# Second attention branch begun ahead of its gate's projections, a pair every eight weight tiles, and five tiles between block transpose and split

## The chip, the cores and the metric

The kernel runs on one core of a Trainium2 chip. The metric is the device time of one execution in microseconds. Three runs of the kernel before took 1014.35, 1013.31 and 1014.84 us (median 1014.35).

## The reference

One decoder layer over 256 tokens of width 2048, in fp32. A normalized input is multiplied by one wide matrix, whose columns feed three gated branches and three merge gates.

```
h = rmsnorm(x, norm_g)
proj = h @ w_in                      # qa ka va ga | qb kb vb gb | xc gc | mg
ya = moba_attention(qa, ka, va)      # branch A: 8 heads of 128, causal over 256
yb = swa_attention(qb, kb, vb)       # branch B: 16 query heads of 64, 4 key heads, window 128, sinks
yc = rglru_branch(xc)                # branch C: convolution, gated linear recurrence
y = [ya * silu(ga), yb * silu(gb), yc * silu(gc)]
merged = sum(sigmoid(mg) * (y[b] @ w_br[b]))
x = x + merged @ w_out
x = x + sigmoid(rmsnorm(x) @ w_pg) * (p @ w_pp)
return rmsnorm(x, final_norm_g)
```

Both attentions add a relative-position bias to their logits. For 256 tokens branch A has one block and so is plain causal attention.

## The kernel before

All weights stream from memory in tiles of 128 x 1024 fp32 (512 KB): 232 of `w_in`, 48 of `w_br`, 32 of `w_out`, 32 of `w_pg`, 4 of `w_pp`. Each product keeps its precision by splitting both operands into a high and a low part: ScalarE casts a tile to the high part (`wh`, L118), VectorE subtracts to get the low part (`wl`, L119), and TensorE multiplies high by high, high by low and low by high (`mm3`, L150 to L152, or L212 and L214 where the output is wanted feature-major). There are four raw tiles and four split tiles, so the cast of a tile waits until TensorE has done with the tile four places earlier, and TensorE runs at most some tiles behind the splits. SyncE issues the weight loads, in order.

The order of the big stages is: branch C's projections, branch A's projections with branch C's recurrence between, the merge of C, branch B's projections, the merge of A, the merge of B, the output projection, the last gate. The small work of the two attentions is not in a stage of its own. It is cut into steps (generators) that `hand_out` (L131) puts on a list, and `tick` (L122) takes one entry from the list after every weight tile that is split. `period` is the number of ticks from one pair of heads to the next, `STEPS` the number of ticks that a pair's generator needs, and `drain` (L127) runs what is left. A scheduler then lays the instructions of each engine in an order; weight splits have a priority ahead of the steps.

A pair of branch B (`pair`, L661) does this, a line for each step:

- step 0: for an even pair, load the bias of four heads (ScalarE's queue) and split keys and values (`head_group`, L647)
- step 1: split the queries (`q_b`, L669 and L670), scores on TensorE (`s_b`, L523)
- step 2: add the bias and take the maximum (L539, L541)
- step 3: exponential on ScalarE (L553), then `AHEAD` = 4 ticks of nothing
- step 7: normalize (L562), transpose in blocks of 32 on VectorE (`flip_b`, L569), send to DRAM (`d_b`, L571) and fetch back as four blocks (`turn_b`, L574) on SyncE, then `LATE` ticks of nothing
- then: split the probabilities (`w_b`, high part on ScalarE L598, low part on VectorE L599) and multiply with the values on TensorE (`py_b`, L523)
- last step: put the heads together (L689, L691), multiply with the gate (L693), split the result (L226, L227)

Branch A's pairs (`pair`, L610) have the same form with a period of 11 ticks over the merge of C (48 tiles), and use the same `LATE` and `STEPS`. Before, branch B's pairs are handed out after its gate's projections (`silu`, L731) with a period of 6, over the 48 tiles of the merge of A, and run into the first tiles of the merge of B. In the merge of A each of four column blocks ends with a product on VectorE (`sg_a`, L792) and an add on GpSimd (`merged`, L793); the next block begins with 8 tiles of `w_in`, then 4 of `w_br`.

Of the kernel before, what the change touches and what calls it, by code (L numbers as in the profile page):

```python
# [28 lines left out]
NB, DB = 16, 64  # L29
# [10 lines left out]
WPAD = 64  # L40
QD = 32
AHEAD = 4
STEPS = 13
LATE = 3
TURN_LATE = 5
WOFF = 32
RV = 384
# [3 lines left out]
def trunk(ctx: ExitStack, tc: tile.TileContext, x, xt, p, table, onehot, maskv, w_in, sinks, conv, w_ri, vec, fin, w_br,  # L51
# [14 lines left out]
    def ktiles(t):  # L66
        return t[:, : KB * SEQ].rearrange("p (k t) -> p k t", k=KB)

    def cols(k, n=1):
        return slice(k * SEQ, (k + n) * SEQ)  # L70

    def aux(name):
        return ps_x.tile([P, CW], F32, tag="aux", name=name)

    def temp(name):
        return small.tile([P, 4, SEQ], F32, tag="tmp", name=name, bufs=4)
# [54 lines left out]
    def hand_out(works, period):  # L131

        end = object()
        live = []

        def step():
            live[:] = [g for g in live if next(g, end) is not end]

        def begin(g):
            live.append(g)  # L140
            step()

        for g in works:
            todo.append(lambda g=g: begin(g))
            todo.extend([step] * (period - 1))
        todo.extend([step] * (STEPS - period))

# [69 lines left out]
    def unit(name):  # L217
        return block(f"{name}_hi", F32R), block(f"{name}_lo", F32R)
# [212 lines left out]
    def bias_tile(h0, n, name):  # L431
        t = small.tile([P, 4, 2 * P], F32, tag="bias", name=name)
        nc.scalar.dma_start(t[:, :n], bass.AP(tensor=rv_d.tensor, offset=rv_d.offset + h0 * RV, ap=[[1, P], [RV, n], [1, 2 * P]]))
        return t
# [9 lines left out]
    def turned(dst, n, factor=None):  # L444
        for c in range(n):
            scaled(dst[:, 2 * c : 2 * c + 2, :], in_turned(), factor)

    def silu(dst, n, name):
        for c in range(0, n, 2):
            d = dst[:, 2 * c : 2 * c + 4, :]  # L450
            turned(d, 2)
            s = temp(f"sig_{name}{c}")
            nc.scalar.activation(s, d, AF.Sigmoid)
            nc.vector.tensor_tensor(d, d, s, op=ALU.mult)
# [61 lines left out]
    def chained(calls):  # L516
        ins = None
        for call in calls:
            with tc.issue_after(ins) if ins is not None else nullcontext():
                ins = call().ins  # L520

    def mm(out, a, b, start, stop):
        return lambda: nc.tensor.matmul(out, a, b, start=start, stop=stop)  # L523

    def probs(name):
        return small.tile([P, 3, 2, P], F32, tag="e", name=name, bufs=2)
# [37 lines left out]
    def flip(dst, srcs, n, name):  # L564

        t = temp(f"flip_{name}").rearrange("p k t -> p (k t)")[:, : n * P]
        view = t.rearrange("p (b m q) -> p m b q", b=4, m=n)
        for at, src in srcs:
            nc.vector.transpose(view[:, at], src.rearrange("p (m b q) -> p m b q", b=4, q=QD))  # L569
        d = dram.tile([P, n * P], F32, tag=f"flip{n}", name=f"d_{name}", bufs=4)  # L570
        nc.sync.dma_start(d, t)  # L571
        back = d.rearrange("(a i) (b c) -> b i a c", a=4, b=4)
        for b in range(4):
            nc.sync.dma_start(dst[quad[b]].rearrange("i (a c) -> i a c", a=4), back[b])  # L574
# [4 lines left out]
    def turned_probs(es, name, out):  # L579
        t = temp(f"turn_{name}").rearrange("p k t -> p (k t)")[:, : 6 * P]  # L580
        flip(t, [(slice(0, 6), es.rearrange("p k j t -> p (k j t)"))], 6, name)
        for _ in range(LATE):
            yield
        out.append(flipped(t, 6))

    def softmax_steps(es, scs, bias, mx, den, name, out, sk=None, sink=None):
        softmax_max(es, scs, bias, mx, sk, sink)
        yield
        softmax_exp(es, mx, den, sk)
        for _ in range(AHEAD):  # L590
            yield
        softmax_norm(es, den, sk)
        yield from turned_probs(es, name, out)

    def split_probs(t, n, name):
        w = small.tile([P, 2, 6 * P], F32R, tag="w", name=name)[:, :, : n * P]
        hi, lo = (w[:, i].rearrange("p (m a q) -> p m a q", m=n, a=4) for i in range(2))
        nc.scalar.copy(hi, t[:, :n])  # L598
        nc.vector.tensor_tensor(lo, t[:, :n], hi.bitcast(F32), op=ALU.subtract)  # L599
        return [w[:, i] for i in range(2)]  # L600

    def by_head(w, n=2):
        return w[:, : n * SEQ].rearrange("p (k j t) -> p j k t", k=n, j=2)
# [37 lines left out]
    def attention_pairs(qb, kb, vt, gate):  # L641
        z = unit("zb")
        mx, den, sk = (small.tile([P, NB, NH], F32, tag=f"st{i}b", name=f"st{i}b", bufs=1) for i in range(3))
        half = [slice(j * DB, (j + 1) * DB) for j in range(2)]
        shared = {}

        def head_group(g):  # L647
            bias = bias_tile(NA + 4 * g, 4, f"bias_b{g}")
            src, own = kb[g // 2][half[g % 2]], g % 2
            ks = small.tile([P, 2, SEQ], F32R, tag="s", name=f"k_b{g}")  # L650
            nc.scalar.copy(ks[half[0], 1, :], src)
            nc.scalar.copy(ks[half[1], 0, :], src)
            for j in range(2):
                nc.vector.tensor_tensor(ks[half[j], j, :], src, ks[half[own], 1 - own, :].bitcast(F32), op=ALU.subtract)
            vs = small.tile([P, NH, 2, DB], F32R, tag="v", name=f"v_b{g}")
            vsrc = vt[:, :, g * DB : (g + 1) * DB]
            nc.scalar.copy(vs[:, :, 0, :], vsrc)
            nc.vector.tensor_tensor(vs[:, :, 1, :], vsrc, vs[:, :, 0, :].bitcast(F32), op=ALU.subtract)
            shared[g] = bias, ks, vs.rearrange("p c s d -> p c (s d)")

        def pair(i):  # L661
            pr = slice(2 * i, 2 * i + 2)
            if i % 2 == 0:
                head_group(i // 2)
            yield
            bias, ks, vc = shared[i // 2]
            qs = small.tile([P, 2, SEQ], F32R, tag="q", name=f"q_b{i}")
            for j in range(2):
                nc.scalar.copy(qs[half[j], j, :], qb[i][half[j]])  # L669
                nc.vector.tensor_tensor(qs[half[1 - j], j, :], qb[i][half[j]], qs[half[j], j, :].bitcast(F32), op=ALU.subtract)  # L670
            scs = [aux(f"s_b{i}{j}") for j in range(2)]
            early = [sc[:, SEQ:].rearrange("p (s t) -> p s t", s=2) for sc in scs]
            chained([mm(scs[j][:, :SEQ], qs[:, j, P:], ks[:, j ^ n, :], n == 0, n == 1) for j in range(2) for n in range(2)]
                    + [mm(early[j], qs[:, j, :P], ks[:, :, :P], True, True) for j in range(2)])
            es = probs(f"e_b{i}")
            yield
            out = []
            yield from softmax_steps(es, scs, bias[:, i % 2 * 2 : i % 2 * 2 + 2], mx[:, pr], den[:, pr], f"b{i}", out,
                                     sk[:, pr], sinkb[:, pr])
            w = split_probs(out[0], 6, f"w_b{i}")  # L680
            py = aux(f"py_b{i}")
            pj = py.rearrange("p (j k t) -> p j k t", j=2, k=2)
            last = [t[:, 4 * P :].rearrange("p (j t) -> p j t", j=2) for t in w]
            chained([mm(pj, vc[:, 0], by_head(w[1 - n]), n == 0, False) for n in range(2)]
                    + [mm(pj[:, :, 1], vc[:, 1], last[1 - n], False, n == 1) for n in range(2)])
            yield
            y = qb[i]
            for j in range(2):
                nc.scalar.copy(y[half[j]], py[half[1 - j], j * SEQ : (j + 1) * SEQ])  # L689
            for j in range(2):  # L690
                nc.vector.tensor_tensor(y[half[j]], py[half[j], j * SEQ : (j + 1) * SEQ], y[half[j]], op=ALU.add)  # L691
            gi = gate[:, cols(i)]
            nc.vector.tensor_tensor(gi, y, gi, op=ALU.mult)  # L693
            split_act(z, i, 1, gi)

        hand_out([pair(i) for i in range(NB // 2)], 6)
        return z

    def token_values(dst, ps, c0):
# [24 lines left out]
    def branch_b():  # L724
        qT, kv, g = block("qb"), block("kvb"), block("gb")
        turned(ktiles(qT), 4, DB ** -0.5)
        kT = ktiles(kv)[:, :2, :]
        vt = ktiles(kv)[:, 2:4, :]
        turned(kT, 1)
        token_values(vt, in_chunk(NKV * DB), 0)  # L730
        silu(ktiles(g), 4, "gb")  # L731

        qb = [ktiles(qT)[:, i, :] for i in range(NB // 2)]
        kb = [kT[:, i, :] for i in range(2)]
        return attention_pairs(qb, kb, vt, g)

    merged = []
    mT = []
# [223 lines left out]
```

## Time and profile before

| | |
|---|---|
| median of three runs | 1014.35 us |
| profiled execution | 1014.71 us, span 1012.9 us |
| mean granted TensorE clock | 0.996 |
| TensorE busy | 995.3 us (98%) |
| VectorE busy | 673.1 us (66%) |
| ScalarE busy | 549.1 us (54%) |
| HBM traffic | 216.4 MB, 214 GB/s over the span |

How to read it: TensorE's matmuls overlap, so the time of one is told by the distance from its start to the next start (about 0.23 us for 512 columns), not by its duration. A number in brackets behind a row is how long the engine stood idle before it and what ended that. A wait on an engine that is not the bottleneck costs nothing unless TensorE later waits for that engine. The stages in this profile: branch A's pairs run from 286 to 431 us, branch B's projections from 431 to 543 us with the gate's 16 tiles from 498.8, the merge of A from 543.4 to 697, the merge of B up to 828 us.

### The profile page before, as it was taken

To read this page: it belongs to the slowest core of one execution; us is meant where nothing else is said; L and a number is where in the kernel's file an instruction comes from. 1 tells how busy PE (TensorE), PEld (TensorE's weight loads), DVE (VectorE), ACT (ScalarE), POOL (GpSimd) and SP (SyncE) were. 2 spreads that over 40 slices of the span, in tenths; PEclk is the share of its full clock that TensorE was granted. 3 is DMA by queue.
4 is the path that set the end of the run, shared out by engine and by line. 5 is a ranking of instruction groups with operands and counts; after the bars stand their busy time and mean duration, and the time that the engine had idled before them with its cause. 6 is when DMAs were issued, how large, how long until landed. Compare 5 with 4: busy or idle time off the path is not lost.

```text
span 1012.9 us, 13571 instructions
## 1 busy us (share of the span) xinstructions
PE 995.3 (98%) x5024; PEld 845.1 (83%) x5024; DVE 673.1 (66%) x993; ACT 549.1 (54%) x767; POOL 15.1 (1%) x14
## 2 busy tenths in 40 slices
PE   9999999999999999999999998999999999999996
PEld 7888888888888888888988877788788888888886
DVE  6766956667867576555456787697656555565764
ACT  8644455557555556544446756766544444454552
POOL 0000000000000000000000001010000000000000
PEclk9999999999999999999999999999999999999999
DMA  9856656554666766666656657867677786779662
GB/s 338 305 190 220 197 187 180 174 177 157 209 208 205 224 209 195 210 198 191 186 190 199 207 188 207 249 190 240 212 238 231 233 283 207 248 259 326 206 192 83
DMA packets 71977, 216.43 MB, mean 214 GB/s; under 512 B 8120, under 2 KB 21352, under 8 KB 71400
## 3 DMA queue, kind: packets, MB, share of 16 engines
q1 hardware_dynamic: 65376, 202.93, 62.3%
q10 hardware_dynamic: 6536, 12.65, 3.6%
q8 instruction: 39, 0.64, 0.3%
q14 instruction: 26, 0.21, 0.1%
HBM read 202.93 MB, written 12.62 MB: 213 GB/s over the span
## 4 chain that ended last, share of the span: by engine, by line
PE 83%; DMA 5%; DVE 5%; issue 2%; ACT 2%; SPq 1%; POOLq 0%; POOL 0%; ACTq 0%; DVEq 0%
PE ps_in L212 21%; PE ps_in L214 11%; PE ps_in L150 8%; PE ps_in L152 8%; PE ps_in L151 8%; DMA turn_b<-d_b 3%; PE ps_out L150 3%; PE ps_out L151 3%; PE ps_out L152 3%; PE ps_pg L151 3%; PE ps_pg L150 3%; PE ps_pg L152 3%; DMA d_b<-flip_b 2%; PE ps_brc L152 1%; PE ps_brc L150 1%
## 5 line engine op out<-in xcount | busy, mean ns | idle before, releaser
L119 DVE TENSOR_TENSOR wl_in<-r_in,wh_in 128x1024 fp32r<-128x1024 f32 x232 | 284.5, 1228 | 177.3 <-ACT wh_in L118 176.8
L118 ACT CAST wh_in<-r_in 128x1024 fp32r<-128x1024 f32 x232 | 242.7, 1049 | 245.8 <-PE ps_in L212 140.6
L212 PE MATMUL ps_in<-h,wh_in 128*128 128x512 f32 x928 | 290.2, 393 | 0.0
L214 PEld LDWEIGHTS ps_in<-h,wl_in 128*128 128x128 f32 x928 | 173.6, 188 | 39.5
L151 PE MATMUL ps_in<-wl_in,h 128*128 128x512 f32 (+1 forms) x480 | 184.1, 383 | 0.6 <-DVE wl_in L119 0.6
L152 PE MATMUL ps_in<-wh_in,h 128*128 128x512 f32 (+1 forms) x480 | 184.4, 384 | 0.0
L214 PE MATMUL ps_in<-h,wl_in 128*128 128x256 f32 x928 | 184.4, 280 | 0.0
L150 PE MATMUL ps_in<-wh_in,h 128*128 128x512 f32 (+1 forms) x480 | 184.3, 384 | 0.0
L212 PEld LDWEIGHTS ps_in<-h,wh_in 128*128 128x128 f32 x928 | 142.5, 188 | 0.4
L151 PEld LDWEIGHTS ps_in<-wl_in,h 128*128 128x128 f32 x480 | 90.5, 189 | 18.4 <-DVE wl_in L119 1.5
L152 PEld LDWEIGHTS ps_in<-wh_in,h 128*128 128x128 f32 x480 | 90.4, 188 | 17.6
L150 PEld LDWEIGHTS ps_in<-wh_in,h 128*128 128x128 f32 x480 | 90.6, 189 | 17.0
L119 DVE TENSOR_TENSOR wl_out<-r_out,wh_out 128x1024 fp32r<-128x1024 f32 x32 | 38.8, 1223 | 25.7 <-ACT wh_out L118 25.7
L119 DVE TENSOR_TENSOR wl_pg<-r_pg,wh_pg 128x1024 fp32r<-128x1024 f32 x32 | 38.9, 1222 | 25.2 <-ACT wh_pg L118 25.0
L151 PE MATMUL ps_pg<-wl_pg,x_hi 128*128 128x512 f32 (+1 forms) x160 | 55.3, 347 | 0.0
L152 PE MATMUL ps_pg<-wh_pg,x_lo 128*128 128x512 f32 (+1 forms) x160 | 55.3, 347 | 0.0
L150 PE MATMUL ps_pg<-wh_pg,x_hi 128*128 128x512 f32 (+1 forms) x160 | 55.3, 347 | 0.0
L118 ACT CAST wh_out<-r_out 128x1024 fp32r<-128x1024 f32 x32 | 33.4, 1051 | 35.9 <-PE ps_out L152 29.9
L118 ACT CAST wh_pg<-r_pg 128x1024 fp32r<-128x1024 f32 x32 | 33.4, 1052 | 32.1 <-PE ps_pg L152 24.7
L150 PE MATMUL ps_out<-wh_out,m_hi 128*128 128x512 f32 x128 | 49.9, 390 | 0.0
L152 PE MATMUL ps_out<-wh_out,m_lo 128*128 128x512 f32 x128 | 49.8, 389 | 0.0
L151 PE MATMUL ps_out<-wl_out,m_hi 128*128 128x512 f32 x128 | 49.8, 389 | 0.0
(250 smaller groups left out, 1237.6 us busy)
## 6 DMA issues: line engine op xcount, KB each, us to landing
r_in<-w_in_dram SPq DMA_DIRECT2D x232, 512.0 KB, 4.2
r_out<-w_out_dram SPq DMA_DIRECT2D x32, 512.0 KB, 4.3
r_pg<-w_pg_dram SPq DMA_DIRECT2D x24, 512.0 KB, 5.1
r_brc<-w_br_dram SPq DMA_DIRECT2D x16, 512.0 KB, 3.6
r_bra<-w_br_dram SPq DMA_DIRECT2D x16, 512.0 KB, 4.1
r_brb<-w_br_dram SPq DMA_DIRECT2D x16, 512.0 KB, 4.7
r_pg<-w_pgt_dram SPq DMA_DIRECT2D x8, 512.0 KB, 3.3
d_b<-flip_b SPq DMA_DIRECT2D x8, 384.0 KB, 3.5
```

Of the source, the lines that this page charges most:

```text
L118: casts.append(nc.scalar.copy(hi[:, c], r[:, c]).ins)
L119: los.append(nc.vector.tensor_tensor(lo[:, c], r[:, c], hi[:, c].bitcast(F32), op=ALU.subtract).ins)
L150: nc.tensor.matmul(ps, ah, bh, start=first, stop=False)
L151: nc.tensor.matmul(ps, ah, bl, start=False, stop=False)
L152: nc.tensor.matmul(ps, al, bh, start=False, stop=last)
L212: nc.tensor.matmul(ps[:, j, :], wh[:, cs[j]], h_both[k], start=k == 0, stop=False)
L214: nc.tensor.matmul(ps[:, j, SEQ:], wl[:, cs[j]], h_act[k][0], start=False, stop=k == KD - 1)
```

## The change

Two numbers change: `STEPS` from 13 to 14 and `LATE` from 3 to 5, so that a pair waits five ticks, not three, from its block transpose to its split; this holds for both attentions. The call of `attention_pairs` stands before the gate's projections `silu(ktiles(g), 4, "gb")`, so the first ticks of branch B's pairs fall in those 16 tiles, and the period of its pairs is 8 ticks, not 6. A pair's last step, which needs the gate, comes 13 ticks after its first, when the gate's first half has been projected.

```diff
-STEPS = 13
-LATE = 3
+STEPS = 14
+LATE = 5
@@ attention_pairs
-        hand_out([pair(i) for i in range(NB // 2)], 6)
+        hand_out([pair(i) for i in range(NB // 2)], 8)
         return z
@@ branch_b
         token_values(vt, in_chunk(NKV * DB), 0)
-        silu(ktiles(g), 4, "gb")
-
         qb = [ktiles(qT)[:, i, :] for i in range(NB // 2)]
         kb = [kT[:, i, :] for i in range(2)]
-        return attention_pairs(qb, kb, vt, g)
+        z = attention_pairs(qb, kb, vt, g)
+        silu(ktiles(g), 4, "gb")
+        return z
```

VectorE before, where pair 2 is transposed at the end of the merge's second block of `w_in` tiles (`wl_bra_0` is the first tile of `w_br` behind them; `w_b_5257` belongs to pair 1, `e_b_5188` and `flip_b_5333` to pair 2, `q_b_5341` to pair 3):

```order
L599 TENSOR_TENSOR w_b_5257<-turn_b_5166,w_b_5257 128x768
L562 TENSOR_SCALAR e_b_5188<-e_b_5188,st1b 128x2x128
L562 TENSOR_SCALAR e_b_5188<-e_b_5188,st1b 128x128
L562 TENSOR_SCALAR e_b_5188<-e_b_5188,st1b 128x2x128
L562 TENSOR_SCALAR e_b_5188<-e_b_5188,st1b 128x128
L670 TENSOR_TENSOR q_b_5341<-qb,q_b_5341 64x256 x2
L119 TENSOR_TENSOR wl_bra_0_5373<-r_bra_0_5370,wh_bra_0_5372 128x1024
L569 STREAM_TRANSPOSE flip_b_5333<-e_b_5188 128x6x4x32
L119 TENSOR_TENSOR wl_bra_1_5400<-r_bra_1_5397,wh_bra_1_5399 128x1024
```

VectorE after, where pair 2 is transposed, now behind the merge's first block (`e_b_4965` and `flip_b_5110` are pair 2's, `py_b_5037` and the gate product `gb` pair 1's, `q_b_5157` pair 3's):

```order
L558 TENSOR_TENSOR st1b<-st1b,st2b 128x4
L559 RECIPROCAL st1b<-st1b 128x4
L562 TENSOR_SCALAR e_b_4965<-e_b_4965,st1b 128x2x128
L562 TENSOR_SCALAR e_b_4965<-e_b_4965,st1b 128x128
L562 TENSOR_SCALAR e_b_4965<-e_b_4965,st1b 128x2x128
L691 TENSOR_TENSOR qb<-py_b_5037,qb 64x256 x2
L562 TENSOR_SCALAR e_b_4965<-e_b_4965,st1b 128x128
L119 TENSOR_TENSOR wl_bra_0_5136<-r_bra_0_5133,wh_bra_0_5135 128x1024
L693 TENSOR_TENSOR gb<-qb,gb 128x256
L569 STREAM_TRANSPOSE flip_b_5110<-e_b_4965 128x6x4x32
L119 TENSOR_TENSOR wl_bra_1_5154<-r_bra_1_5151,wh_bra_1_5153 128x1024
L670 TENSOR_TENSOR q_b_5157<-qb,q_b_5157 64x256 x2
```

Before, the split of pair 1, the normalization of pair 2 and the query split of pair 3 stand between two weight splits; after, pair 1's split is gone from there, its last step stands there instead, and pair 3's query split comes after the transpose.

TensorE before, where it comes to pair 2's values (`wh_in_0_5477` is the tile whose low part stands right before pair 2's split on VectorE):

```order
L150 MATMUL ps_in_5474<-wh_in_0_5477,h_116 128x512
L151 MATMUL ps_in_5474<-wl_in_0_5478,h_116 128x512
L523 MATMUL py_b_5429<-w_b_5426,v_b_5139 128x512 x2
L523 MATMUL py_b_5429<-w_b_5426,v_b_5139 128x2x128 x2
L152 MATMUL ps_in_5474<-wh_in_0_5477,h_116 128x512
```

TensorE after, where it comes to pair 2's values (`wh_in_0_5239` is again the tile whose low part stands before pair 2's split on VectorE, `wh_bra_3` the tile before it):

```order
L151 MATMUL ps_bra_5132<-wl_bra_3_5213,za_hi 128x512
L152 MATMUL ps_bra_5132<-wh_bra_3_5212,za_lo 128x512
L523 MATMUL py_b_5246<-w_b_5243,v_b_4931 128x512 x2
L523 MATMUL py_b_5246<-w_b_5243,v_b_4931 128x2x128 x2
L150 MATMUL ps_in_5236<-wh_in_0_5239,h_116 128x512
L151 MATMUL ps_in_5236<-wl_in_0_5240,h_116 128x512
```

The values of pair 2 move from five matmuls inside that tile to ahead of its first matmul, four tiles behind the tile of the transpose.

SyncE before, at the round trip of pair 2 (`d_b` goes to DRAM, `turn_b` comes back):

```order
L103 DMA r_in_0_5475<-w_in_dram 128x1024
L571 DMA d_b_5335<-flip_b_5333 128x768
L103 DMA r_in_1_5503<-w_in_dram 128x1024
L103 DMA r_in_2_5550<-w_in_dram 128x1024
L574 DMA turn_b_5332<-d_b_5335 32x4x192 x4
L103 DMA r_in_3_5577<-w_in_dram 128x1024
```

SyncE after, at the round trip of pair 2:

```order
L103 DMA r_in_0_5237<-w_in_dram 128x1024
L571 DMA d_b_5112<-flip_b_5110 128x768
L103 DMA r_in_1_5263<-w_in_dram 128x1024
L574 DMA turn_b_5109<-d_b_5112 32x4x192 x4
L103 DMA r_in_2_5288<-w_in_dram 128x1024
L103 DMA r_in_3_5306<-w_in_dram 128x1024
```

One weight load, not two, stands between the way out and the way back.

## Rows read from the trace of the kernel before

**Rows 1.** The page's list of engines: busy time, share of the span, instructions.

```profile
PE 995.3 (98%) x5024; PEld 845.1 (83%) x5024; DVE 673.1 (66%) x993; ACT 549.1 (54%) x767; POOL 15.1 (1%) x14
```

**Rows 2.** Waits of TensorE: who waited for whom, us in total, times, longest.

```profile
PE py_b L523 <- DVE w_b L599: 6.1, 4, 2.5
```

**Rows 3.** Windows: stretch, us, busy time by engine, granted clock, DMA share, GB/s.

```profile
286.20:431.50 145.30, 145.30 (x687) 121.87 (x686) 93.03 (x152) 85.01 (x132) 0.00 (x0) 1.00 0.65 207
...
498.90:543.40 44.50, 44.50 (x258) 38.94 (x257) 26.50 (x28) 21.72 (x28) 0.00 (x0) 1.00 0.61 201
...
543.40:718.90 175.50, 168.52 (x754) 137.40 (x753) 136.06 (x286) 113.60 (x202) 11.69 (x4) 0.99 0.68 213
...
660.00:663.00 3.00, 3.00 (x12) 2.57 (x11) 2.91 (x7) 2.92 (x6) 0.00 (x0) 0.50 0.41 119
...
718.93:751.57 32.64, 32.64 (x146) 27.04 (x144) 19.29 (x17) 16.04 (x16) 0.00 (x0) 1.00 0.72 222
```

**Rows 4.** Timeline of TensorE: start us, us, line, operation, tiles, [idle before].

```profile
577.12 0.85 PE L523 MATMUL py_b<-w_b,v_b 128*128 128x512 f32 x4
577.80 0.40 PE L151 MATMUL ps_bra<-wl_bra,za_hi 128*128 128x512 f32 x1
...
581.00 0.88 PE L523 MATMUL s_b<-k_b,q_b 128*128 128x256 f32 x6
581.72 0.39 PE L150 MATMUL ps_in<-wh_in,h 128*128 128x512 f32 x1
...
604.87 0.39 PE L150 MATMUL ps_bra<-wh_bra,za_hi 128*128 128x512 f32 x1
...
616.65 0.39 PE L151 MATMUL ps_in<-wl_in,h 128*128 128x512 f32 x1
619.58 0.93 PE L523 MATMUL py_b<-w_b,v_b 128*128 128x512 f32 x4 [2.54 <-DVE w_b L599]
...
727.09 0.39 PE L150 MATMUL ps_brb<-wh_brb,zb_hi 128*128 128x512 f32 x1
```

**Rows 5.** The chain that ended last, pair 2's round trip: start us, us, what.

```profile
603.97 0.98 DVE flip_b L569
...
604.97 3.91 DMA d_b<-flip_b
...
610.25 7.29 DMA turn_b<-d_b
```

**Rows 6.** Timeline of VectorE.

```profile
582.42 2.97 DVE L562 TENSOR_SCALAR e_b<-e_b,st1b 128x256 f32<-128x256 f32 x3
...
602.82 1.23 DVE L119 TENSOR_TENSOR wl_bra<-r_bra,wh_bra 128x1024 fp32r<-128x1024 f32 x1
...
618.47 0.96 DVE L599 TENSOR_TENSOR w_b<-turn_b,w_b 128x768 fp32r<-128x768 f32 x1 [5.61 <-ACT w_b L598]
...
623.90 0.80 DVE L562 TENSOR_SCALAR e_b<-e_b,st1b 128x256 f32<-128x256 f32 x3
...
698.96 0.97 DVE L569 STREAM_TRANSPOSE flip_b<-e_b 128x768 f32<-128x768 f32 x1
...
709.10 0.96 DVE L599 TENSOR_TENSOR w_b<-turn_b,w_b 128x768 fp32r<-128x768 f32 x1 [2.59 <-ACT w_b L598]
...
720.26 1.22 DVE L119 TENSOR_TENSOR wl_brb<-r_brb,wh_brb 128x1024 fp32r<-128x1024 f32 x1 [1.49 <-ACT wh_brb L118]
```

**Rows 7.** Groups of VectorE, 543.4 to 718.9: count, busy us, mean ns, idle before.

```profile
L119 DVE TENSOR_TENSOR wl_in<-r_in,wh_in 128x1024 fp32r<-128x1024 f32 x37 | 46.6, 1263 | 11.9 <-ACT wh_in L118 11.7
L119 DVE TENSOR_TENSOR wl_bra<-r_bra,wh_bra 128x1024 fp32r<-128x1024 f32 x16 | 19.1, 1211 | 0.4 <-ACT wh_bra L118 0.3
```

**Rows 8.** Timeline of ScalarE and its queue.

```profile
609.63 0.40 ACTq L433 DMA_DIRECT2D bias_b<-rv_d  x1
...
610.91 1.28 ACT L550 ACT_TABLE_LOAD   x1
```

**Rows 9.** Timeline of GpSimd.

```profile
582.65 2.39 POOL L793 TENSOR_TENSOR merged<-merged,sg_a 128x1024 f32<-128x1024 f32 x1 [526.56 <-DVE sg_a L792]
```

## The prediction

> **What bounds the kernel now.** I read the page's list of engines first: TensorE is busy 98% of the span [rows 1], so only a stretch where it waits or is slow can give time back. The view of waits for TensorE then names one place, the second branch's `py_b` products waiting for the lower half of the split probabilities, L599: 6.1 us in four waits [rows 2]. The windows say how much the whole stretch loses [rows 3]. A quiet stretch holds 12 weight tiles in 32.64 us, 2.72 us a tile, with no pair in it. From 543.4 to 718.9 TensorE passes 56 tiles (48 of the merge with branch A, 8 of the next) and the eight pairs. A pair costs it 0.72 us for the scores (581.00 to 581.72) and 0.68 us for the values (577.12 to 577.80) where nothing waits [rows 4]. 56 x 2.72 + 8 x 1.40 = 163.5 us; the row says 175.5 us. So 12.0 us are lost there, and that is the most this change can win. Branch A's stretch (286.2 to 431.5) has TensorE busy for all of its 145.30 us, so nothing can be won there.
>
> The 12.0 us are made up so. The four waits: 6.1 us idle, and each has 0.16 us more from start to start than its idle (616.65 to 619.58 is 2.93, less the usual 0.23 between starts, against 2.54 idle) [rows 4], together 6.7 us. From 660 to 663 the granted clock is 0.50, the lower of its two levels, right after a wait that ended at 658.4 [rows 3]: 1.5 us. The rest, 3.8 us by difference, is refilling behind waits and short waits for weight and query splits.
>
> Why `py_b` waits: the chain shows pair 2's block transpose on VectorE at 603.97, its way to DRAM 3.91 us, its way back 7.29 us from 610.25 [rows 5]; ScalarE and VectorE then split, until 619.43 [rows 6]. I call the time from the transpose's end (604.94) to the split's end the need: 14.5 us here, 10.1 us for pair 7 (699.93 to 710.06) [rows 6]. The eight, read in the same way, are 12.2, 12.1, 14.5, 11.5, 13.8, 10.5, 11.9, 10.1. Against it stands VectorE's lead: the last weight split ahead of pair 2's transpose ended at 604.05 and TensorE began that tile at 604.87 [rows 4, 6], a lead of 0.8 us. In the quiet stretch a split ends at 721.48 and TensorE begins the tile at 727.09: 5.6 us.
>
> **The change part by part.** *The order.* It does not show more distance: four weight splits stand on VectorE between `flip_b` and the split of the same pair, before and after, and TensorE comes to `py_b` four tiles after the tile whose split precedes the transpose, where before it was 4.4 tiles for pair 2. What the order does change is the heap: before, one pair's split, the next pair's normalization and the third's query split stand in a row ahead of `flip_b`; after, the normalization and transpose share their place only with two small ends of the previous pair. So the gain must come through the lead.
>
> *The lead.* VectorE's work for a pair: 136.06 us busy in the stretch, less the weight splits 46.6 + 19.1 and four merge products of about 1.2 each (as large as a weight split), over eight: 8.2 us [rows 3, 7]. Every six tiles TensorE needs 6 x 2.72 + 1.40 = 17.7 us and VectorE 6 x 1.26 + 0.6 + 8.2 = 16.4 us: 1.3 us spare, so what one late DMA takes is not won back before the next. Every eight tiles it is 23.2 against 8 x 1.26 + 0.8 + 8.2 = 19.1 us: 4.1 us spare. In the gate's projections, where the pairs now begin, VectorE is busy 26.50 of 44.5 us for 16 tiles; one and a half pairs add 12.3 us, and TensorE's share of them about 2.1: 38.8 of 46.6, again some 17% free. So I expect the lead to be near 5.6 us at each transpose.
>
> *The window.* The transpose ends about 1.4 us after its weight split (a gate product of 0.4 and 0.97 for itself). From there to `py_b` TensorE has the lead, four tiles and one score block: 5.6 + 10.9 + 0.7 - 1.4 = 15.8 us. That covers every need, 14.5 included. ScalarE may still stand at the split until the DMA lands, with the next weight cast behind it; at full lead that cast has some 3 us in hand. It was so in branch A before, with no wait on TensorE. The worst needs of before fell on pairs 2 and 4; with pair 2's way back a 512 KB bias load was in flight, issued at 609.63 [rows 8]; after, the bias load stands near the odd pairs' transposes, ahead of their way back. On SyncE one weight load, not two, stands between a pair's way out and back.
>
> *What remains.* GpSimd adds the merged product four times in this stretch, and VectorE is held meanwhile: three normalizations took 2.97 us beside the add of 2.39 us, and 0.80 us without one [rows 6, 9], 2.2 us more. In the new order the transposes of pairs 3 and 6 come about two tiles behind such a product, and their window falls to about 15.8 - 2.2 - 0.5 (half of a key split ahead of them) = 13.1 us against needs of 10.1 to 14.5: 0 to 1.4 us each, and nothing for the other six. I take 1.2 us in all, with short waits included; from 0 to 3 us.
>
> The Trainium skill, SBUF — State Buffer, section "SBUF: two separate sides", speaks against this place: a GpSimd instruction and a VectorE one with two operands in SBUF lock each other out for the whole instruction. By that rule the hold is the whole 2.39 us for the weight split that now follows the product, and pairs 3 and 6 would wait up to 2 x (14.5 - 12.9) = 3.2 us, which gives 1005.5 us. The trace agrees that there is a hold, with 2.2 us.
>
> *At no cost.* Branch A's split comes two tiles later and then stands in the same tile as the next pair's query and key splits; VectorE is busy 93.03 of 145.30 us there, so a heap of about 1 us beyond a tile is covered by the lead. Uncovered, three heaps cost 3 us; gaining there is excluded since TensorE never waits. Pair 4's end, at step 14, is step 47 of 48. ScalarE gets two more table loads at 1.28 us each [rows 8], in the gate's projections, where it is busy 21.72 of 44.5 us. TensorE's attention products only move. The last pair's values stand in the same tile as before.
>
> **The sum.** 12.0 - 1.2 = 10.8 us off. The profiled execution took 1014.71 us with a span of 1012.9, which is 0.36 above the median of the runs, 1014.35. So 1003.9 by its own time, and 1003.6 us against the median.
>
> **Rivals.** *Half the lead.* Late DMAs keep the lead near 2.5 us; the window is 12.7 us, and of the eight needs two exceed it, by 1.8 and 1.1 us. With 2.4 for the two held transposes and some 1.3 of refilling 6.6 us stay lost: 1009.0 us. For it: a way back took 7.29 us [rows 5], and the need varies by 4.4. Against it: 4.1 us spare.
>
> *No lead.* The order has the same distances, so if the lead stays at 0.8 the window is 11.0 us: the needs exceed it by 1.2 + 1.1 + 3.5 + 0.5 + 2.8 + 0.9 = 10.0, and the six waits add 0.16 each: 11.0 of 12.0 stay, 1013.3 us. For it: before had 4.4 tiles and still waited. Against it: VectorE has 18% free.
>
> *Slower.* The same lack of lead, with every pair's way back as slow as pairs 2 and 4: place, the DRAM round trip; price, 8 x (2.8 to 3.5) + 1.3 = 24 to 29 us lost in place of 12.0, so 1026 to 1031 us. It decides from a mean need of 12.3 us at a lead of 0.8 (8 x 1.34 + 1.3 = 12.0). For it: four tiles are fewer than 4.4. Against it: both the lead and the bias loads' place.
>
> **How the numbers follow.** Forecast 65%, half the lead 20%, no lead 10%, slower 5%. The forecast's own range is 1002.0 to 1006.5: 12.0 us and a little timing noise below, 3 us of residual and 2 us of heaps above; with half the lead, the range goes to 1009.2. About 0.2%, 2 us, is what a measurement of this kernel can tell from no change. Faster takes the first two cases and a little of the third: 0.86; the same 0.09; slower 0.05.
>
> **What would show it.** Right: TensorE's waits for L599 fall from 6.1 us to under 1.5; the stretch of 16 + 56 tiles holds about 210 us in place of 220.0; the granted clock stays 1.0 around the pairs; VectorE's weight splits end 4 to 5.6 us ahead of TensorE at the transposes. Wrong: waits on L599 at most pairs, or new ones inside the gate's projections or at branch A's scores, and a lead of about 1 us at the transposes. If only the waits behind the GpSimd adds remain, the residual was mis-sized and nothing else.

## The result, and the profile after

The changed kernel took 1003.00 us (median of four runs, 1002.78 to 1003.21), the kernel before 1013.83 us in the same comparison (four runs). The ratio is 0.9893, with a 95% interval of 0.9875 to 0.991. The forecast was 1003.6 us.

The profiled execution took 1002.9 us with a span of 1001.1 us, so the span is 11.8 us shorter. The page's list of engines after, to be laid beside [rows 1]:

```profile
PE 991.3 (99%) x5024; PEld 845.1 (84%) x5024; DVE 677.0 (68%) x993; ACT 552.1 (55%) x769; POOL 16.4 (2%) x14
```

The view of waits of TensorE holds a single line, which belongs to the kernel's first matmuls, 1 us after its start; the line of [rows 2] is gone:

```profile
PE busy L313 <- DVE ones L81: 1.1, 1, 1.1
```

Windows of the changed kernel (columns as in [rows 3]): the gate's 16 tiles, which begin at 498.39 here and now hold the first pairs, the 56 tiles behind them, 12 quiet tiles, and the piece that was at half clock before:

```profile
498.39:545.20 46.81, 46.81 (x274) 41.13 (x273) 35.34 (x73) 32.09 (x55) 0.00 (x0) 1.00 0.65 203
545.20:707.11 161.91, 161.91 (x739) 134.73 (x737) 129.91 (x238) 105.96 (x173) 12.99 (x4) 1.00 0.69 224
707.11:739.80 32.69, 32.69 (x146) 27.08 (x145) 19.20 (x17) 14.67 (x15) 0.00 (x0) 1.00 0.69 214
660.00:663.00 3.00, 3.00 (x15) 2.46 (x15) 2.91 (x5) 1.36 (x2) 0.00 (x0) 1.00 0.87 284
```

The 72 tiles and eight pairs take 46.81 + 161.91 = 208.7 us, 220.1 before (498.79 to 718.93). TensorE is busy for all of it, and the clock is 1.00 throughout. Without any loss they would take 16 tiles as before, 44.6, and 163.5 for the rest, as the prediction worked it out: 0.6 us are left over, where it was 12.0.

ScalarE, in the stretch from 498 to 730 us, does stand at the split of every pair until the DMA has landed (us in total, times, longest), and nobody on TensorE notices:

```profile
ACT w_b L598 <- DMA turn_b<-d_b: 18.1, 8, 3.5
```

Pair 3 shows how, on VectorE (first fence) and on TensorE (second):

```profile
582.07 1.22 DVE L119 TENSOR_TENSOR wl_in<-r_in,wh_in 128x1024 fp32r<-128x1024 f32 x1
583.20 2.36 DVE L558 TENSOR_TENSOR st1b<-st1b,st2b 128x4 f32<-128x4 f32 x1
...
589.70 0.98 DVE L569 STREAM_TRANSPOSE flip_b<-e_b 128x768 f32<-128x768 f32 x1
...
599.31 0.96 DVE L599 TENSOR_TENSOR w_b<-turn_b,w_b 128x768 fp32r<-128x768 f32 x1 [1.15 <-ACT w_b L598]
```

```profile
603.34 0.85 PE L523 MATMUL py_b<-w_b,v_b 128*128 128x512 f32 x4
```

The transpose ends at 590.68, the split at 600.27: a need of 9.6 us. TensorE comes for it at 603.34, 12.7 us behind the transpose (the window), and does not wait. The same reading for all eight pairs:

| pair | 0 | 1 | 2 | 3 | 4 | 5 | 6 | 7 |
|---|---|---|---|---|---|---|---|---|
| need before | 12.2 | 12.1 | 14.5 | 11.5 | 13.8 | 10.5 | 11.9 | 10.1 |
| window before (its wait taken off) | 13.8 | 11.6 | 12.1 | 11.7 | 12.1 | 12.4 | 13.3 | 9.3 |
| need after | 11.9 | 10.9 | 10.3 | 9.6 | 10.9 | 12.5 | 10.3 | 10.0 |
| window after | 16.4 | 14.8 | 14.1 | 12.7 | 14.3 | 15.8 | 12.6 | 12.2 |

Before, four pairs had a window shorter than their need; after, every window is at least 2.2 us longer than its need.

### The profile page after: what moved, and what is told of

Read it like the earlier page. It is cut to its first block, busy times and chain, and to the rows that moved or that the text cites. A ratio compares the mean times of both kernels' runs of the same rounds, so it can differ in the third digit from the quotient of the medians.

```text
span 1001.1 us, 13563 instructions
## 1 busy us (share of the span) xinstructions
PE 991.3 (99%) x5024; PEld 845.1 (84%) x5024; DVE 677.0 (68%) x993; ACT 552.1 (55%) x769; POOL 16.4 (2%) x14
## 4 chain that ended last, share of the span: by engine, by line
PE 99%; issue 0%; DVE 0%; POOLq 0%; POOL 0%; ACT 0%; DVEq 0%
PE ps_in L212 21%; PE ps_in L214 11%; PE ps_in L150 11%; PE ps_in L151 11%; PE ps_in L152 11%; PE ps_out L152 3%; PE ps_out L151 3%; PE ps_out L150 3%; PE ps_pg L151 3%; PE ps_pg L150 3%; PE ps_pg L152 3%; PE ps_bra L151 1%; PE ps_brc L150 1%; PE ps_brc L152 1%; PE ps_bra L150 1%; PE ps_bra L152 1%
```

## The experiments

Two ideas were tested against each other. *Distance and lead:* TensorE must come to a pair's values later than the round trip needs, which takes weight tiles between transpose and split, and a VectorE that is ahead. *Heap:* what matters is what else stands in the tick of the split, and how full VectorE is. "Stretch" is from branch B's first weight product to the merge of B's first (`ps_brb`): 287.4 us before, 276.0 after. "Tiles" is the number of weight splits that stand on VectorE between a pair's transpose and its split in the order as laid out. The stretch is that of the one profiled execution, the time the median of all.

| run | period, place | tiles | stretch, us | time, us | ratio to before, 95% |
|---|---|---|---|---|---|
| before | 6, behind the gate | 4 (3 in two pairs) | 287.4 | 1013.8 | 1 |
| late_only | 6, behind the gate | 3 (4 in two) | 291.9 | 1018.7 | 1.0033, 1.002 to 1.0045 |
| late_three | 8, ahead of it | 3 (4 in one) | 292.4 | 1019.4 | 1.004, 1.0022 to 1.0058 |
| late_four | 8, ahead of it | 3 | 287.7 | 1015.9 | 1.0015, 1.0004 to 1.0026 |
| move_only | 6, ahead of it | 3 | 281.9 | 1014.3 | 0.9997, 0.9979 to 1.0015 |
| move_late | 6, ahead of it | 3 and 4 | 281.2 | 1009.8 | 0.9943, 0.9926 to 0.996 |
| same_ticks | 8, ahead of it | 4 (3 in one) | 276.3 | 1004.2 | 0.9899, 0.9884 to 0.9914 |
| after | 8, ahead of it | 4 | 276.0 | 1003.0 | 0.9893, 0.9875 to 0.991 |
| late_six | 8, ahead of it | 5 | 276.0 | 1003.4 | 0.9888, 0.9867 to 0.9908 |

The time of move_only scattered from 1009.7 to 1019.3 us in ten runs, and the profiled one was its fastest, so its stretch flatters it; that of move_late, too, is from its fastest. The tiles do not order the table by themselves: move_only has three in every pair and is no slower than before, late_three has three or four and is slower. The ratios of runs that were not sent together have each their own runs of before under them, whose median went from 1013.8 to 1016.5 us from one comparison to the next.

### The parts of the change by themselves

late_only is the kernel before with

```diff
-STEPS = 13
-LATE = 3
+STEPS = 14
+LATE = 5
```

> Only the five ticks between block transpose and split (LATE 5, STEPS 14); period 6 and the place of the pairs as before. Theory 1, the lead: VectorE keeps 1.3 us spare a pair, so its lead stays about 1 us and most of the loss stays, 1009 to 1015 us, TensorE's waits for L599 4 to 7 us. Theory 2, the distance: two more ticks cover the round trip, the waits vanish, 1002 to 1005 us. The order leans to the first: the scheduler puts the transpose itself later, so that it still stands three or four weight splits ahead of the split.

It was slower. TensorE's waits:

```profile
PE py_b L523 <- DVE w_b L599: 4.7, 3, 3.3
PE ps_in L151 <- DVE wl_in L119: 4.6, 6, 1.1
```

Five ticks at a period of six put the split into the tick in which the next pair but one begins, and in the order as laid out there were fewer weight splits between transpose and split than before, three, and not more. `LATE` counts ticks; what a pair gets for them is settled by the order.

late_three is the changed kernel with `STEPS = 13`, `LATE = 3`.

> The changed kernel with three ticks again between transpose and split (LATE 3, STEPS 13); period 8 and the early place stay. In its order TensorE comes to the values 2.2 to 4.0 tiles after the transpose's tile, about 1.1 tiles or 3 us sooner than in the changed kernel. Theory 1, the lead: windows of 12.2 to 16.4 us shrink to about 9.3 to 13.4 us against needs of 9.6 to 12.5, so some pairs wait 1 to 2 us; 3 to 6 us lost, 1006 to 1009 us. Theory 2, the distance: everything was the two ticks, all is lost again, 1012 to 1015 us.

Both missed: 1019.4 us, the slowest of all. TensorE's waits, then the hold of ScalarE in sum, then ScalarE at pair 3, are:

```profile
PE py_b L523 <- DVE w_b L599: 5.7, 2, 3.2
PE py_b L523 <- DVE st0b L544: 3.7, 2, 3.1
```

```profile
ACT w_b L598 <- DMA turn_b<-d_b: 36.9, 8, 9.2
```

```profile
595.17 1.05 ACT L118 CAST wh_bra<-r_bra 128x1024 fp32r<-128x1024 f32 x1 [0.33 <-PE ps_in L152]
605.41 0.83 ACT L598 CAST w_b<-turn_b 128x768 fp32r<-128x768 f32 x1 [9.19 <-DMA turn_b<-d_b]
606.15 1.04 ACT L118 CAST wh_bra<-r_bra 128x1024 fp32r<-128x1024 f32 x1
```

ScalarE comes to the split 9.19 us too early and stands there, and the next weight cast stands behind it in its queue: 10 us pass without one, TensorE works off all that was split, and VectorE's lead is gone for the following pair as well. (The longer of the waits put down to `st0b` is the same one: VectorE's split ended at 607.24, and TensorE began at 607.38.) The granted clock falls in the stretches with these waits:

```profile
620.00:660.00 40.00, 37.44 (x165) 30.57 (x164) 28.99 (x61) 24.85 (x41) 3.23 (x1) 0.96 0.71 223
700.00:735.00 35.00, 31.79 (x134) 25.83 (x133) 17.84 (x19) 14.98 (x18) 3.24 (x1) 0.95 0.64 204
```

move_only is the changed kernel with `STEPS = 13`, `LATE = 3` and the period 6 again; move_late is the changed kernel with the period 6 alone.

> Only the place: the pairs begin ahead of the gate's projections, with period 6 and three ticks as before. Theory 1, the lead: VectorE has no more spare time a pair than before, and in the gate's projections none at all (26.5 us of its own and 2.7 pairs of 8.2 in some 48 us), so 1011 to 1018 us with waits for L599 or for weight splits. Theory 3, the place: an earlier start is what counts, 1003 to 1006 us.

> The changed kernel with period 6: early place and five ticks, but pairs as dense as before. Theory 1, the lead: 1008 to 1015 us, TensorE waits 3 us or more in all. Theory 2, the distance, or 3, the place: 1002 to 1005 us with no waits.

The place alone is worth nothing that can be measured; with the five ticks it is worth half. So the parts don't give shares that add up: the five ticks without the move make the kernel slower, and so does the move with its period without the five ticks. At the early place the four runs also show what the period does: from 6 to 8 the time rises from 1014.3 to 1019.4 us with three ticks and falls from 1009.8 to 1003.0 with five. With three ticks, more room for VectorE did not help.

### Distance or heap

late_three left it open whether the short distance was at fault or the ticks on which the split now fell (beside the next pair's maximum and exponential). same_ticks keeps those ticks and gives the five ticks back, by an earlier transpose:

```diff
-AHEAD = 4
-STEPS = 14
+AHEAD = 2
+STEPS = 13
```

> The changed kernel with its block transpose two ticks earlier (AHEAD 2, not 4; STEPS 13; LATE 5 stays). A pair's split and last step then fall on the same ticks of the next pair (2 and 3, beside maximum and exponential) as in the run with LATE 3 at period 8, which took 1019.4 us; but the five ticks between transpose and split stay. Distance theory (LATE 3 was slow since ScalarE came to the split before the round trip had landed and held the next weight casts): 1002.5 to 1006 us, holds of ScalarE on turn_b of 3 us or so as in the changed kernel, not 6 to 9. Heap theory (it was slow since the split and the last step fell on the busy ticks): 1014 to 1020 us, with waits of 3 us or more on L599.

1004.2 us, and TensorE has no wait in the stretch. ScalarE's hold (498 to 730 us) is short again:

```profile
ACT w_b L598 <- DMA turn_b<-d_b: 20.9, 8, 4.7
```

Distance stands, the heap on these ticks falls. What the ticks move can be read on ScalarE. In pair 3 of late_three (first fence, with its casts above) the transpose ended at 596.21 and ScalarE stood at the split from 596.22; in pair 3 of the changed kernel (second fence), with the transpose's end at 590.68, it came to the split 5.0 us behind it:

```profile
595.23 0.98 DVE L569 STREAM_TRANSPOSE flip_b<-e_b 128x768 f32<-128x768 f32 x1
```

```profile
598.45 0.83 ACT L598 CAST w_b<-turn_b 128x768 fp32r<-128x768 f32 x1 [2.77 <-DMA turn_b<-d_b]
```

The DMA frees ScalarE at about the same distance from the transpose in both kernels, 8.0 to 9.7 us over the pairs of late_three and 7.8 to 10.7 after. But ScalarE comes to the split 0.0 to 7.5 us behind the transpose in late_three, within 2.2 us in four pairs, and 5.0 to 8.9 us behind it after. late_four (changed kernel, `STEPS = 13`, `LATE = 4`) was to lie between.

> The changed kernel with LATE 4 and STEPS 13, so one tick less between transpose and split than it has, one more than the run at 1019.4 us; the split falls on the tick of the next pair's exponential. Distance theory: the longest holds of ScalarE fall by one tile, 2.7 us, from 9.2 to about 6.5 us; a full lead of 5.6 us covers most of it, so 1004 to 1010 us. Heap theory: the split beside the exponential is the worst place, 1014 to 1020 us.

It did not; the distance theory missed by 6 us as it was put. TensorE's waits, and ScalarE's hold:

```profile
PE py_b L523 <- DVE w_b L599: 7.1, 4, 3.2
```

```profile
ACT w_b L598 <- DMA turn_b<-d_b: 39.7, 8, 9.0
```

The hold is as long as with three ticks. The order, read after the result, accounts for it: with four ticks the split still stands three weight splits behind the transpose, in all eight pairs, as it does in seven pairs with three ticks, and only the fifth tick makes it four. ScalarE again comes to the split within 1.6 us of the transpose in four pairs. late_six (`STEPS = 15`, `LATE = 6`) has five.

> The changed kernel with LATE 6 and STEPS 15, one tick more between transpose and split (five weight splits between them in the order, where the changed kernel has four and the runs with LATE 3 and 4 had three). Theory that what counts is the distance in weight tiles as laid out, up to the point where the round trip is covered: nothing more to gain, 1002.5 to 1004 us, the holds of ScalarE on turn_b under 10 us in all in place of 18.1. Heap theory (the split beside the pair's last step is what moves the time): 1006 us or more.

As the distance theory said: nothing more to be had. Its windows are 15.2 to 19.4 us against needs of 10.4 to 14.7 (the need grows when the split is reached later, since it is taken up to the split's end), and ScalarE, which comes to the split 8.2 to 12.4 us behind the transpose, hardly stands there at all.

### The lead

three_buffers is the changed kernel with one split weight tile less.

```diff
-    wsp = ctx.enter_context(tc.tile_pool(name="wsp", bufs=4))
+    wsp = ctx.enter_context(tc.tile_pool(name="wsp", bufs=3))
```

> The changed kernel with three split weight tiles in place of four, in the whole program, so VectorE can be one tile (2.7 us) less ahead of TensorE. Lead theory: the windows of the changed kernel (12.2 to 16.4 us) shrink by 2.7 each, and against its needs (9.6 to 12.5) pairs 6 and 7 come out 0.4 and 0.5 us short; with refilling, and heaps elsewhere that the lead covered, 1004 to 1009 us and waits on L599 or L119 of 1 to 5 us. Theory that distance in ticks alone counts: 1002.5 to 1003.5 us and no waits.

1011.5 us (ratio 0.997, 0.9959 to 0.9982), which is 8 us more than after, but not where the theory put it. Its stretch took 276.0 us and held no wait of TensorE. Its waits stand in other stages, and of the 9.2 us that its span is longer 3.2 are lost ahead of branch B and 6.0 behind the stretch:

```profile
PE ps_out L151 <- DVE wl_out L119: 1.9, 3, 0.8
PE ps_in L214 <- DVE wl_in L119: 1.8, 3, 0.9
```

The order was also laid anew: TensorE now comes to `py_b` almost a tile later than in the changed kernel, so the windows stayed 12.3 to 15.9 us although VectorE's lead at the transposes of pairs 2 to 7 fell to between 0 and 1.9 us. This run doesn't tell what the lead alone is worth. What it shows is that distance can stand in for it.

### The bias loads

The prediction blamed a 512 KB bias load for the long needs of pairs 2 and 4. bias_ahead is the kernel before with these loads taken early.

```diff
+        ahead = [bias_tile(NA + 4 * g, 4, f"bias_b{g}") for g in range(3)]
...
-            bias = bias_tile(NA + 4 * g, 4, f"bias_b{g}")
+            if g == 1:
+                ahead.append(bias_tile(NA + 12, 4, "bias_b3"))
+            bias = ahead[g]
```

> The kernel before, with branch B's bias loads issued ahead of the first pairs (three bias buffers; the fourth load with the second head group), so that hardly one is in flight beside the round trips of pairs 2 and 4. Theory that those loads made the needs of pairs 2 and 4 long (14.5 and 13.8 us): their needs fall to 10 to 12, their waits of 2.54 and 1.87 us go, and the time is 1008.5 to 1011.5 us. Rival (the weight loads in the same queue and the heap make them long): 1013 to 1015 us, the waits stay.

The needs of pairs 2 and 4 fell as the theory said, to 12.1 and 10.4 us, and their waits to 0 and 0.7. But the time was 1016.0 us, slower than before (ratio 1.0015, 1.0005 to 1.0024), and the waits stand elsewhere:

```profile
PE py_b L523 <- DVE w_b L599: 4.9, 5, 1.5
PE ps_in L151 <- DVE wl_in L119: 3.2, 4, 1.4
```

The order again: with the load gone, the split stands two to three weight splits behind the transpose from pair 3 on, and the windows of pairs 3 to 7 fell to 8.9 to 9.9 us. So the run fits the bias load as a cause of the long needs, though it does not isolate it, and it shows that a shorter need is worth nothing when the order gives the gain away.

### Without the round trip

no_round_trip is the kernel before with branch B's probabilities split straight from the transpose. (`flip_{name}` is the transposed tile, which the split then reads.)

```diff
+        if name.startswith("b"):
+            t = temp(f"flip_{name}").rearrange("p k t -> p (k t)")[:, : 6 * P]
...
+            nc.vector.transpose(view, src.rearrange("p (m b q) -> p m b q", b=4, q=QD))
```

> The kernel before, with branch B's probabilities split straight from the block transpose: the way to DRAM and back is left out, so branch B's values are computed from blocks in the wrong places; branch A keeps its round trip. The split then comes one to three weight splits behind the transpose, not four, since the order is laid anew. Theory that the 12 us lost in the merge of A come from waiting for that round trip and its filling up again: the waits for L599 go and the stretch loses at most 2 us, 1002.5 to 1004.5 us. Rival, the heap (normalization, transpose, splits of three pairs in a row on VectorE every six tiles are the loss, the DMA only stands at its end): VectorE stays behind, waits on L119 and L599 of 4 us or more, 1008 to 1013 us.

1008.9 us (ratio 0.9943, 0.9922 to 0.9963), stretch 281.4 us: about half of what the change wins, and the rival's number. Its chain at pair 3, on GpSimd, VectorE, ScalarE and TensorE:

```profile
621.59 3.24 POOL L799 TENSOR_TENSOR merged<-merged,sg_a 128x1024 f32<-128x1024 f32 x1 [34.03 <-DVE sg_a L798]
```

```profile
621.36 1.22 DVE L119 TENSOR_TENSOR wl_in<-r_in,wh_in 128x1024 fp32r<-128x1024 f32 x1
622.49 2.62 DVE L227 TENSOR_TENSOR zb_lo<-gb,zb_hi 128x256 fp32r<-128x256 f32 x1
625.03 0.96 DVE L584 STREAM_TRANSPOSE flip_b<-e_b 128x768 f32<-128x768 f32 x1
```

```profile
626.03 0.83 ACT L604 CAST w_b<-flip_b 128x768 fp32r<-128x768 f32 x1 [5.37 <-DVE flip_b L584]
626.77 1.99 ACT L118 CAST wh_in<-r_in 128x1024 fp32r<-128x1024 f32 x2
```

```profile
628.25 0.50 PE L151 MATMUL ps_in<-wl_in,h 128*128 128x512 f32 x1 [2.04 <-DVE wl_in L119]
```

VectorE is held 2.2 us at a small split that takes 0.42 us elsewhere, while GpSimd adds; the transpose behind it is late, ScalarE stands at a split that is now laid one to three weight splits behind the transpose, the weight casts stand behind that, and TensorE waits. no_trip_no_add puts the merge's adds on VectorE as well:

```diff
-            (nc.vector if bi == 2 else nc.gpsimd).tensor_tensor(dst, dst, sg, op=ALU.add)
+            nc.vector.tensor_tensor(dst, dst, sg, op=ALU.add)
```

> The run without the round trip (1008.9 us, two waits of 2 us for weight splits), with the merge's four adds on VectorE (about 1.2 us each) in place of GpSimd (3.24 us each, during which a VectorE instruction was held 2.2 us longer than its 0.4). Theory that the hold behind the add is what starts the waits that are left: VectorE wins 1 us at each add, the longest wait falls from 2.0 to under 1, 1004.5 to 1007 us. Rival (VectorE has too little to spare at a pair every six tiles, whatever holds it): no change, 1008 to 1010 us.

1003.4 us (ratio 0.9872, 0.9848 to 0.9897), more than either theory allowed: a stretch of 276.0 us, the same as after, at the old place and with a pair every six tiles. In the window that held the wait of 2.04 us VectorE is busier than in the run before it (18.34 of the 20 us there), and TensorE does not wait:

```profile
620.00:640.00 20.00, 20.00 (x93) 16.70 (x92) 18.75 (x44) 13.11 (x24) 0.00 (x0) 1.00 0.56 174
```

So, without the round trip, VectorE's load is not what costs the time. Late arrivals are: the round trip in the kernel before, the add's hold once the order has moved it ahead of a transpose. Both runs also laid the order anew, so they do not price the round trip of the kernel before by itself. Whether the adds on VectorE would help the kernel before with its round trip in place was not tried.

after_no_trip is the changed kernel with the same part left out.

> The changed kernel with the same left out (branch B's probabilities split straight from the block transpose). If the changed kernel already hides the whole round trip, nothing is to be had: 1002.5 to 1003.3 us. If something is still lost behind the holds of ScalarE (18 us in eight) that the view of waits does not show: 1000.5 to 1002 us.

1003.3 us, stretch 276.0 us: the changed kernel hides the whole round trip, and 276.0 us is the shortest stretch of any run. The need, read as above, is still 8.6 to 12.0 us although no DMA stands in it. So in the changed kernel it is set mostly by where the order puts the split, and the table of needs and windows shows that TensorE came late enough, not what the DMA took.

## Why the prediction was right, and where its steps were not

**What could be won.** 12.0 us was the bound, the stretch became 11.4 us shorter, and its 276.0 us are what five different runs (after, late_six, after_no_trip, no_trip_no_add, three_buffers) come down to. The reading of the windows against a quiet stretch found the size of the loss; the 6.1 us of waits alone would have given half of it.

**The lead.** The step as put, "near 5.6 us at each transpose", was too high. Counted tile by tile, VectorE's lead at the transposes of pairs 2 to 7 is 3.7, 2.8, 3.5, 5.0, 2.2 and 2.2 us, where before it was 0.8, 1.7, 0.8, 2.4, 2.1 and 3.4. So the windows are 12.2 to 16.4 us, not 15.8 for six pairs and 13.1 for two. Pairs 3 and 6 are short, as forecast; pair 7, the shortest, was not named.

**The needs.** They were taken as they stood, up to 14.5 us. They fell to 9.6 to 12.5. This error and the one before cancel, which is luck: the windows of pairs 3, 6 and 7, 12.2 to 12.7 us, would not have covered a need of 13.8 or 14.5. That the bias loads now stand elsewhere was named as a help and given no price. Over pairs 2 to 7 the mean window grew by 1.8 us and the mean need fell by 1.5, so nearly half of what TensorE gained on the splits came from a term that the sum left out. Why the needs fell is open: the bias loads, the loads on SyncE and the place of the split moved together. The distance on ScalarE did not grow: it came to the split 5.6 to 10.4 us behind the transpose before and 5.0 to 8.9 us after; the longest that the DMA held it was until 12.7 us behind the transpose before, 10.7 after.

**The residual.** The mis-sized term: 1.2 us were forecast for waits behind the GpSimd adds and short waits, and there is no wait at all on `py_b`. The 0.6 us that are left over hold no wait of TensorE either, and the run without the adds on GpSimd has the same stretch, so they may be an error of the 163.5 us and not a loss. That 1003.0 us came so near to 1003.6 says little about this term: the kernel before scattered from 1013.1 to 1014.8 us in the same comparison, and its median there, 1013.83, was 0.5 us below the one that the forecast started from. The hold itself came as it was read, 2.36 us where 0.16 would do, ahead of pair 3's transpose (583.20, above), and ahead of pair 6's too.

**The five ticks.** The prediction said that the order shows no more distance and that the gain must come through the lead, and it costed the new `LATE` at nothing. The first half was right (four splits before and after), but the conclusion left the main thing out: at a period of eight, three or four ticks are worth three splits, and then the same move is slower by up to 0.4%. The five ticks keep the distance that the move would have lost.

**The spare of VectorE.** 1.3 us per pair at a period of six was called the reason why a late DMA is not won back. no_trip_no_add loses nothing at that period, so the spare suffices when nothing comes late. move_only and move_late, with a period of six in the new place, do lose; there the distance is three tiles in some or all pairs. The period by itself went both ways in the runs, 5.1 us slower at eight with three ticks and 6.8 us faster with five. With five the order also went from three or four tiles to four throughout, so what the spare alone is worth stays open.

**At no cost.** Branch A's stretch has TensorE busy throughout, as in [rows 3]; ScalarE's table loads and its 18.1 us of holds show nowhere on TensorE. The clock stays at its upper level where a wait had been followed by 3 us at 0.50 before.

**The rivals.** Half the lead came true as a lead, at 2.2 to 5.0 us, but not as a time, since the needs had shrunk. (Its 2.4 us for the two held transposes have no working: 12.7 less 2.7 is a window of 10.0, against needs of 11.5 and 11.9, so 3.4 us and 1010.0 in place of 1009.0.) No lead and the slower case did not occur in the changed kernel; late_three is their picture: a round trip that is not covered, at a lead of 0.1 us for pairs 4 and 7. What the lead alone is worth no run shows.

## What to carry to other kernels

A wait in an in-order queue costs what stands behind it: look, in the order as laid out and not in the parameter, at when the engine that needs a transfer comes to its instruction, and compare that with the transfer's worst duration. Here that engine was ScalarE. Knobs that set such an order do not add up, so that parts which are slower alone can be right together; an experiment that takes something out should have its new order read before its time is. The excess of a stretch over the same tiles in a quiet one was here a better bound for the gain (12.0 us, of which 11.4 came) than the sum of the waits that the profile names (6.1 us).

## What the runs showed of the hardware

In these runs a GpSimd add of 128 x 1024 fp32 and VectorE instructions with two operands in SBUF excluded each other. Behind an add, a VectorE instruction of 0.16 us took 2.36 us and one of 0.42 us took 2.62, 2.2 us more in both. A normalization, which reads a tile and a column of factors, was held as long ([rows 6], 2.97 us for three in place of 0.80). The add in turn took 3.25 us where its record begins beside a weight split in progress (582.30 in the kernel after, with the split from 582.07 to 583.29), and 2.39 us in [rows 9], beside a short instruction. Transposes and instructions that read PSUM passed beside an add at their usual durations. The second add of the kernel before, which had a weight split to wait for from 625.95 to 627.17, shows it: the product that reads `py_b` and the transpose both ran while it did.

```profile
625.99 3.45 POOL L793 TENSOR_TENSOR merged<-merged,sg_a 128x1024 f32<-128x1024 f32 x1 [40.94 <-DVE sg_a L792]
```

```profile
627.09 0.85 DVE L691 TENSOR_TENSOR qb<-py_b,qb 64x256 f32<-64x256 f32 x2
627.97 0.98 DVE L569 STREAM_TRANSPOSE flip_b<-e_b 128x768 f32<-128x768 f32 x1
```

So the price of an add depends on what the order puts behind it. That is the lock that the Trainium skill describes (SBUF — State Buffer, section "SBUF: two separate sides"), and the trace agrees with it more closely than the prediction granted: the instruction of 2.36 us ended at 585.56, with the add (582.30 and 3.25 us). But ahead of pairs 3 and 6 it was not the weight split behind the product that paid, as the prediction had it by that rule: the split began before the add, and the add waited for it.
